# Loading and transposing the first four row tiles in halves of the contraction, under a new plan

## Chip, cores, metric

One core of one Trainium2 chip. The time is device microseconds (us) of one execution; lower is better. The kernel before takes 316.13 us (median of 4 runs, 315.47 to 316.74).

## The reference

```python
# x: 16 x 512 x 1024, w1 and w2: 1024 x 768, all float32
def reference(x, w1, w2):
    y1 = np.matmul(x, w1)
    y2 = np.matmul(x, w2)
    return (np.tanh(y1) * y2).astype(np.float32)
```

## The kernel before

The 64 row tiles (128 rows each) are worked in two ways. The first six, the *head*, are multiplied directly while the weights still arrive. The other 58 go in 29 pairs (numbered 0 to 28) through a scheme with seven block products in place of eight; that is the *steady part*, which begins at about 44 us. Its x tiles are loaded, cast and transposed by the DMA (a *transposing transfer*). A plan in the kernel fixes the order of the work on each engine and in the DMA queue that SyncE issues ("dma"). In the plan `Lx0` loads row tile 0, `La0` a row block of w1, `T00` and `T01` transpose the two halves of tile 0 on TensorE, `m00F3` is a head product, `st0` stores a head tile, `Lp70`, `Tx70` load and transpose the first tile of pair 7, `store0.5` stores a steady result, `p1.0` and so on are steady products.

```python
    WARM = 21                     # filler matmuls while the first loads run
    LOADS = ("x0 a0 x1 a1 x2 a2 x3 a3 a4 a5 a6 a7 b0 b1 b2 b3 b4 b5 b6 b7").split()
    EARLY = ("La0", "La1", "La2", "La3")      # issued by ACT, the rest by SyncE
    FILL = {"m00F0": 3, "m00F1": 6}           # fillers on ones, ahead of these
    ORDER = {
        "pe": """
            T00 T01 m00F0 m00G0 T10 T11 m00F1 m00G1 m10F0 T20 m10G0 m10G1 m10F1 T21 ...
        """,
        # ... "act", "dve" ...
        "dma": """
            Lx0 La0 Lx1 La1 Lx2 La2 Lx3 La3 La4 La5 La6 La7 Lb0 Lb1 Lb2 Lb3 Lb4 Lx4 Lb5 Lb6 Lx5 Lb7 Lp00 Lp01
            Lp10 Lp11 Tx00 Lp20 Tx01 st3 Lp21 Tx10 Lp30 st4 Tx11 Lp31 st1 Tx20 Lp40 Lp41 Tx21 st2 Lp50 Tx30
            Lp51 Tx31 Lp60 st5 Tx40 Lp61 st0 Tx41 Lp70 store1.5 Tx50 store0.5 Lp71 Tx51 store0.1 store1.1 Tx60
            store0.7 store1.7 Tx61 store1.3 store0.3 store0.9 store1.9
        """,
    }
    # ...
    def load_head_x(mt, h=None):
        if mt not in hf:
            hf[mt] = xfpool.tile([P, K], f32, tag="xf", name="x_f")
        cols = slice(0, K) if h is None else slice(h * K // 2, (h + 1) * K // 2)
        pin(nc.sync.dma_start(hf[mt][:, cols], xf[mt][:, cols]))
    # ...
    # past the plan, by slots of 0.65 us (one product):
    for i in range(FIRST, PAIRS):
        z = 14 * i - 6
        # ...
        late = 1.1 * (i == FIRST + 1)
        for h in range(2):
            at(slot(z - 24 + (1 + h) * late + 4 * h), cast_x, i, h, "dve")
            at(slot(z - 24 + (1 + h) * late + 4 * h), transpose_x, i, h)
```

Of the kernel before, what the change touches and what calls it, by code (L numbers as in the profile page):

```python
# [13 lines left out]
def kernel(  # L14
# [739 lines left out]
```

## Time and profile before

| | before |
|---|---|
| span of the profiled run | 314.2 us |
| first transposition on TensorE | 6.21 us |
| first steady product | 43.94 us |
| TensorE lost between there and 46.63 (worked out in the prediction) | 0.75 us |
| idle TensorE from 46.63 to 310.5 | 0.03 us |

TensorE is the bound, so the table is read as a sum: when does the steady part begin, and what does TensorE wait for from there on? The lines are in the prediction below.

### The profile page before, as it was taken

The page shows a single profiled execution, that of the slowest core. Times are in us where ns is not written, and L with a number is a line of the kernel's source. Part 1 is how long each engine was busy: PE and PEld are TensorE (multiplying, and loading weights), DVE is VectorE, ACT ScalarE, POOL GpSimd, SP SyncE. Part 2 cuts the span into 40 slices and gives each one's busy share as a digit, 9 for nine tenths or more (in the row PEclk, how much of TensorE's full clock was granted, in tenths as well). Part 3 has the DMA queues.
Part 4 walks back from the last instruction along what each step waited for, and adds up shares of the span by engine and source line. Part 5 has one row for each costly group of instructions (what it writes and reads, how often), then busy time and mean ns, then how long its engine had stood idle before and what let it go on. Part 6 is the DMA issues. An engine that isn't in the chain of part 4 may idle for free.

```text
span 314.2 us, 5489 instructions
## 1 busy us (share of the span) xinstructions
PE 307.3 (98%) x1893; PEld 185.6 (59%) x1898; DVE 244.8 (78%) x571; ACT 230.5 (73%) x453; POOL 4.3 (1%) x10
## 2 busy tenths in 40 slices
PE   7999999999999999999999999999999999999995
PEld 5756656666656555555555556555555555555662
DVE  1688988888788778877777887777788777778653
ACT  3798879787888777778777777877777787776552
POOL 0000000000000000000000000000000000000004
PEclk9999999999999999999999999999999999999999
DMA  7999398999999999999999989999998989985322
GB/s 276 407 399 381 78 310 237 271 299 258 290 288 310 297 272 231 228 294 266 285 240 252 273 253 225 291 252 259 253 251 281 260 256 271 237 256 126 144 103 100
DMA packets 82300, 80.59 MB, mean 256 GB/s; under 512 B 63584, under 2 KB 64096, under 8 KB 82272
## 3 DMA queue, kind: packets, MB, share of 16 engines
q1 hardware_dynamic: 81552, 78.46, 88.0%
q10 hardware_dynamic: 720, 1.77, 1.4%
q8 instruction: 15, 0.25, 0.3%
q14 instruction: 13, 0.11, 0.1%
HBM read 39.85 MB, written 25.17 MB: 207 GB/s over the span
## 4 chain that ended last, share of the span: by engine, by line
PE 89%; DMA 8%; DVE 1%; issue 1%; ACT 0%; ACTq 0%; SPq 0%; DVEq 0%
PE bank L401 84%; DMA wf<-in_w_dram 8%; PE bank L267 3%; PE bank L270 2%; DVE t L318 1%; DVE s L382 1%; PE bank L238 0%; DVE o L437 0%; ACT o L283 0%; ACTq L250 0%; SPq L250 0%; ACT junk L260 0%; PE bank L300 0%; DVE o L287 0%; DVE out_r L390 0%
## 5 line engine op out<-in xcount | busy, mean ns | idle before, releaser
L401 PE MATMUL bank<-t,s 128*128 128x384 f16 x696 | 131.5, 326 | 0.4 <-DVE t L318 0.4
L401 PEld LDWEIGHTS <-s 128*128 128x128 f16 x928 | 90.7, 98 | 61.1 <-issue 0.8
L401 PEld LDWEIGHTS <-xT 128*128 128x128 f16 x696 | 68.0, 98 | 46.7 <-issue 0.9
L401 PE MATMUL bank<-b,xT 128*128 128x384 f16 x464 | 93.7, 326 | 0.0
L423 DVE TENSOR_TENSOR c<-bank,u 128x384 f32<-128x384 f32 x58 | 31.9, 553 | 41.1 <-PE bank L401 39.6
L340 ACT ACTIVATE junk<-x_f 128x1024 bf16<-128x1024 f32 x58 | 60.8, 1049 | 2.4 <-DMA x_f<-in_x_dram 2.4
L431 ACT ACTIVATE th<-c,out_r 128x384 f32<-128x384 f32 x58 | 35.3, 609 | 21.1 <-DVE c L423 21.1
L401 PE MATMUL bank<-b,s 128*128 128x384 f16 x232 | 47.0, 326 | 0.0
L401 PE MATMUL bank<-t,xT 128*128 128x384 f16 x232 | 46.9, 325 | 0.0
L418 ACT ACTIVATE u<-bank 128x384 f32<-128x384 f32 x58 | 28.2, 487 | 20.0 <-PE bank L401 19.7
L360 DVE TENSOR_SCALAR x_h<-x_f,pr 128x1024 f16<-128x1024 f32 x55 | 41.0, 746 | 0.2
L431 ACT ACTIVATE th<-bank,out_r 128x384 f32<-128x384 f32 x58 | 33.3, 574 | 6.1 <-PE bank L401 6.1
L414 ACT ACTIVATE bank<-bank 128x384 f32<-128x384 f32 x58 | 27.9, 481 | 12.6 <-DVE o L437 10.0
L437 DVE SCALAR_TENSOR_TENSOR o<-bank,out_r,th 128x384 f32<-128x384 f32 x58 | 35.4, 610 | 2.0 <-PE bank L401 2.0
L423 DVE TENSOR_TENSOR c<-bank,s 128x384 f32<-128x384 f32 x58 | 32.1, 554 | 6.1 <-PE bank L401 5.0
L437 DVE SCALAR_TENSOR_TENSOR o<-c,out_r,th 128x384 f32<-128x384 f32 (+1 forms) x57 | 34.3, 606 | 0.4 <-ACT th L431 0.2
L418 ACT ACTIVATE s<-bank 128x384 f32<-128x384 f32 x58 | 27.9, 482 | 7.3 <-PE bank L401 5.1
L382 DVE TENSOR_TENSOR s<-xT 128x512 f16<-128x512 f16 x58 | 24.0, 416 | 0.2
L267 PE MATMUL bank<-wb,xTb 128*128 128x512 bf16 x91 | 23.6, 379 | 0.1
L270 PE MATMUL bank<-wb,xTb 128*128 128x256 bf16 x96 | 14.6, 273 | 0.1
L260 ACT ACTIVATE junk<-wf 128x768 bf16<-128x768 f32 (+1 forms) x13 | 12.8, 988 | 1.4 <-DMA wf<-in_w_dram 1.2
L267 PEld LDWEIGHTS <-xTb 128*128 128x128 bf16 x96 | 9.3, 99 | 7.5 <-DVE xTb L231 0.3
(49 smaller groups left out, 143.4 us busy)
## 6 DMA issues: line engine op xcount, KB each, us to landing
x_f<-in_x_dram SPq DMA_DIRECT2D x64, 512.0 KB, 5.8
out_dram<-o SPq DMA_DIRECT2D x62, 384.0 KB, 3.6
wf<-in_w_dram SPq DMA_DIRECT2D x12, 384.0 KB, 7.7
wf<-in_w_dram ACTq DMA_DIRECT2D x4, 384.0 KB, 8.5
xT<-x_h SPq DMA_TRANSPOSE x58, 3.7
out_dram<-o SPq DMA_DIRECT2D x3, 192.0 KB, 1.9
out_dram<-o ACTq DMA_DIRECT2D x1, 192.0 KB, 1.9
```

The costliest lines, as they stand in the source:

```text
L260: pin(nc.scalar.activation(junk[:, :n * N].rearrange("p (k n) -> p k n", n=N), w_f[t][:, k:k + n, :], ACT.Abs, accum_out=asum_w[t][:, j:j ...
L267: pin(nc.tensor.matmul(bank, hx[mt][:, k, :], w_b[t][k][:, :F], start=k == 0, stop=k == KO - 1))
L270: pin(nc.tensor.matmul(bank[:, at_:at_ + G], hx[mt][:, k, :], w_b[t][k][:, F:], start=k == 0 and mt % 2 == 0, stop=k == KO - 1, skip_group ...
L340: pin(nc.scalar.activation(junk[:, :K], xs[HEAD + 2 * i + h], ACT.Abs, scale=2.0 ** -12, accum_out=pair_sum[i][:, h:h + 1]))
L360: pin(nc.vector.tensor_scalar(xh, xs.pop(mt), pair_r[i][:, h:h + 1], None, ALU.mult))
L382: pin((nc.vector if eng == "dve" else nc.gpsimd).tensor_tensor(s, st[i, a], st[i, b], op))
L401: pin(nc.tensor.matmul(bank[:, cols], st[i, a][:, k, :], wt[t][b][:, k, cols], start=start and k == 0, stop=stop and k == KH - 1, skip_gro ...
L414: pin(nc.scalar.activation(ub[u]["b"][:, :Q], ub[u]["a"][:, :Q], ACT.Copy))
L418: pin(nc.scalar.activation(c, ub[u][bank][:, :Q], ACT.Copy))
L423: pin(nc.vector.tensor_tensor(c, ub[u][bank][:, :Q], ub[u][other], ALU.add))
L431: pin(nc.scalar.activation(th, v, ACT.Tanh, scale=rs[i][:, 0, h:h + 1]))
L437: pin(nc.vector.scalar_tensor_tensor(o[:, h, q * Q + cols.start:q * Q + cols.stop], v, rs[i][:, 1, h:h + 1], tanhs[i, h, q][:, cols], ALU. ...
```

## The change

The intent: a row tile's load of 512 KB becomes two of 256 KB, one for each half of the contraction, and the four first halves are loaded ahead of the four second ones. TensorE can then transpose and multiply first halves with the first weight blocks about 0.7 us earlier. A new plan for all engines and for the DMA queue comes with it. The diff, cut to its core:

```diff
-    WARM = 21
+    WARM = 15
-    LOADS = ("x0 a0 x1 a1 x2 a2 x3 a3 a4 a5 a6 a7 b0 b1 b2 b3 b4 b5 b6 b7").split()
+    LOADS = ("x00 a0 x10 a1 x20 a2 x30 a3 x01 a4 x11 a5 x21 a6 x31 a7 b0 b1 b2 b3 b4 b5 b6 b7").split()
-    FILL = {"m00F0": 3, "m00F1": 6}
+    FILL = {"T10": 5, "T20": 3}
     "pe":
-            T00 T01 m00F0 m00G0 T10 T11 m00F1 m00G1 m10F0 T20 m10G0 m10G1 m10F1 T21 ...
+            T00 T10 m00F0 m00G0 T20 m10F0 m10F1 m10G0 m10G1 T30 m00G1 m00F1 T01 m00F2 m10G2 m00G2 m10F2 m20F0
+            T11 m20F1 m20G0 m20F2 m20G1 m20G2 m20G3 m20F3 T21 ...
     "act", around the start of the steady part:
-            ... tanh4G ax20 cx11 b11b b22b seed.0 seed.1 s5.0 u2.0 ax21 ...
+            ... tanh4G b22b b11b cx11 seed.0 ax21 s5.0 seed.1 u2.0 ax20 ...
     "dma":
-            ... Tx00 Lp20 Tx01 st3 Lp21 Tx10 Lp30 st4 Tx11 Lp31 st1 Tx20 Lp40 Lp41 Tx21 st2 Lp50 Tx30 ...
+            ... Tx00 Lp20 Tx01 Lp21 st0 Tx10 st4 Lp30 Tx11 Lp31 Tx20 Lp40 Lp41 Tx21 Lp50 st1 Tx30 ...
     # (other lines of the plan, the dependencies of the halves: cut)
-            pin(nc.tensor.transpose(banks[6 + h][:, k * P:(k + 1) * P],
+            pin(nc.tensor.transpose(banks[6 + mt % 2][:, k * P:(k + 1) * P],
-            op(f"L{what}", "dma", STEP[what], n - 200, [], load_head_x, i)
+            op(f"L{what}", "dma", STEP.get(what, 0.72), n - 200, [], load_head_x, i, int(what[2]))
```

More of the change, by code (lines that the diff above doesn't have):

```diff
@@ L58 @@
     ELSEWHERE = {
-        "e01": "dve", "e11": "dve", "e20": "act", "e21": "dve", "e31": "dve", "ca0": "act", "ca1": "act",
-        "cb4": "act", "b22a": "dve", "cx11": "act", "cx31": "act", "cx61": "act"
+        "e10": "act", "e21": "dve", "e31": "dve", "cb4": "act", "b22a": "dve", "cx11": "act", "cx31":
+        "act", "cx41": "act", "cx61": "act"
     }
-    FILL = {"m00F0": 3, "m00F1": 6}
+    FILL = {"T10": 5, "T20": 3}
     ORDER = {
         "pe": """
-            T00 T01 m00F0 m00G0 T10 T11 m00F1 m00G1 m10F0 T20 m10G0 m10G1 m10F1 T21 m20G0 m20F0 m20F1 m20G1
-            m10G2 m20G2 m00F2 m00G2 m20F2 m10F2 T30 T31 m10G3 m00G3 m20F3 m10F3 m20G3 m00F3 m10F4 m10G4 m20F4
-            m20G4 m00G4 m00F4 m30G0 m30G1 m30G2 m30G3 m20G5 m10G5 m10F5 m20F5 m20G6 m10G6 m10F6 m30G4 m30G5
-            m30G6 m20G7 m10G7 m30G7 m10F7 m00F5 m00F6 m00F7 suma m11F0 m20F6 m20F7 m01F0 m00G5 m00G6 m00G7
-            m11F1 m01F1 m30F0 m30F1 m30F2 m30F3 m30F4 m30F5 m30F6 m30F7 m21F0 m21F1 m11F2 m21F2 m01F2 m11F3
-            m21F3 m01F3 m31F0 m31F1 m31F2 m31F3 m21G0 m21G1 m21G2 m21G3 m31G0 m31G1 m31G2 m31G3 m01F4 m31G4
-            m21G4 m11F4 m01G0 m01G1 m11G0 m11G1 m01G2 m01G3 m01G4 m31F4 T4 m11F5 m11F6 m01F5 m31F5 m01G5 m01G6
-            m31F6 m01F6 m31G5 m31G6 m01F7 m31F7 m11F7 m31G7 T5 m40F0 m40F1 m40F2 m40F3 m40F4 m40F5 m40F6 m01G7
-            m40F7 m21G5 m21G6 m50F0 m50F1 m50F2 m50F3 m50F4 m50F5 m50F6 m50F7 m21F4 m21F5 m21G7 m21F6 m21F7
-            m11G2 m11G3 m11G4 m11G5 m11G6 m11G7 m40G0 m50G0 m50G1 m50G2 m50G3 m50G4 m50G5 m50G6 m50G7 m40G1
-            m40G2 m40G3 m40G4 m40G5 m40G6 m40G7 sumb m41F0 m41F1 m41F2 m41F3 m41F4 m41F5 m41F6 m41F7 m41G0
-            m41G1 m41G2 m41G3 m41G4 m41G5 m41G6 m51G0 m51G1 m51G2 m51G3 m51G4 m51G5 m51G6 m51G7 m41G7 m51F0
-            m51F1 m51F2 m51F3 m51F4 m51F5 m51F6 m51F7 p1.0 p1.1 p5.0 p6.0 p2.0 p3.0 p7.0 p5.1 p6.1 p4.0 p2.1
-            p7.1 p1.2 p3.1 p4.1 p1.3 p6.2 p2.2 p5.2 p6.3 p2.3 p5.3 p7.2 p7.3 p3.2 p4.2 p3.3 p4.3 p1.4 p1.5
-            p5.4 p5.5 p2.4 p6.4 p6.5 p2.5 p7.4 p7.5 p3.4 p3.5 p4.4 p4.5 p1.6 p1.7 p5.6 p6.6 p2.6 p6.7 p2.7
-            p7.6 p3.6 p5.7 p7.7 p4.6 p3.7 p1.8 p4.7 p1.9 p2.8 p6.8 p5.8 p5.9 p7.8 p1.10 p3.8 p4.8 p3.9 p6.9
@@ new lines @@
+            T00 T10 m00F0 m00G0 T20 m10F0 m10F1 m10G0 m10G1 T30 m00G1 m00F1 T01 m00F2 m10G2 m00G2 m10F2 m20F0
+            T11 m20F1 m20G0 m20F2 m20G1 m20G2 m20G3 m20F3 T21 m00G3 m00F3 m10F3 m10F4 m00F4 m20G4 m00G4 m20F4
+            T31 m30G0 m30G1 m30G2 m30G3 m00G5 m00F5 m20G5 m30G4 m30G5 m00F6 m20G6 m00G6 m30G6 m30G7 m20G7
+            m00G7 m10G3 m10G4 m10F5 m10F6 m10F7 m10G5 suma m20F5 m10G6 m10G7 m30F0 m20F6 m20F7 m11F0 m11F1
+            m11F2 m01F0 m01F1 m01F2 m31F0 m31F1 m31F2 m00F7 m30F1 m30F2 m30F3 m30F4 m30F5 m30F6 m30F7 m11F3
@@ new lines @@
+            m11F4 m01F3 m01F4 m31F3 m21G0 m31G0 m21G1 m21G2 m21G3 m21G4 m01G0 m01G1 m01G2 m01G3 m01G4 m11G0
+            m11G1 m21F0 m21F1 m21F2 m21F3 T4 m21F4 m21G5 m01G5 m01G6 m01F5 m11F5 m01F6 m01F7 m21G6 m21G7 m11G2
+            m11G3 m11G4 m11G5 m11G6 m31G1 m31G2 m31G3 m40F0 m40F1 m21F5 m21F6 m21F7 m11F6 m11F7 T5 m31F4 m31F5
+            m31F6 m31F7 m40F2 m40F3 m40F4 m40F5 m40F6 m40F7 m50F0 m50F1 m50F2 m50F3 m50F4 m50F5 m40G0 m40G1
+            m40G2 m50G0 m11G7 m01G7 m50F6 m50F7 m40G3 m40G4 m40G5 m40G6 m40G7 m31G4 m31G5 m50G1 m50G2 m50G3
@@ new lines @@
+            m50G4 m50G5 m50G6 m50G7 sumb m41F0 m41F1 m41F2 m41F3 m41F4 m41F5 m41F6 m41F7 m31G6 m31G7 m41G0
+            m41G1 m51G0 m41G2 m41G3 m41G4 m41G5 m41G6 m41G7 m51G1 m51G2 m51G3 m51G4 m51G5 m51G6 m51G7 m51F0
+            m51F1 m51F2 m51F3 m51F4 p1.0 p1.1 p5.0 p2.0 p6.0 p5.1 m51F5 m51F6 p6.1 p7.0 p3.0 p7.1 p4.0 m51F7
+            p3.1 p2.1 p4.1 p1.2 p1.3 p5.2 p5.3 p6.2 p2.2 p6.3 p2.3 p7.2 p7.3 p3.2 p4.2 p3.3 p4.3 p1.4 p1.5
+            p5.4 p6.4 p2.4 p2.5 p6.5 p5.5 p7.4 p7.5 p3.4 p4.4 p3.5 p4.5 p1.6 p1.7 p5.6 p5.7 p6.6 p2.6 p6.7
@@ L81 @@
+            p2.7 p7.6 p7.7 p3.6 p4.6 p3.7 p4.7 p1.8 p1.9 p5.8 p6.8 p2.8 p5.9 p7.8 p1.10 p3.8 p4.8 p3.9 p6.9
             p2.9 p2.10 p7.9 p5.10 p4.9
@@ L83 @@
         "act": """
-            ca0 absa0 ca1 absa1 e20 absa2 absa3 absa4 absa5 absa6 absa7 tanh2G absb0 tanh1F tanh0G tanh2F cb4
-            tanh0F absb2 absb6 tanh3F absb4 ax00 absb7 ax01 b21a tanh4F tanh5F ax10 ax11 tanh4G ax20 cx11 b11b
-            b22b seed.0 seed.1 s5.0 u2.0 ax21 b21b u2.1 f00.0 s5.1 f10.0 ax31 seed.2 ax30 seed.3 f11.0 u2.2
-            u2.3 s5.2 s5.3 f00.2 f01.0 ax40 cx31 f10.2 seed.4 ax41 seed.5 s5.4 s5.5 u2.4 u2.5 f11.2 f00.4 ax51
-            f01.2 ax50 f10.4 seed.6 f11.4 seed.7 f01.4 u2.6 s5.6 ax61 u2.7 s5.7 f00.6 f11.6 f10.6 seed.8 ax60
@@ L89 @@
-            f00.8 u2.8 f01.6 s5.8 cx61 s5.9 seed.9 f10.8 seed.10 u2.9 f01.8 f11.8 f00.10 s5.10
+            absa0 e10 absa1 absa2 e01 absa3 e11 absa4 absa5 absa6 absa7 tanh2G absb0 tanh0G b21a cb4 tanh2F
+            tanh0F tanh1F absb2 absb4 absb7 tanh3F ax00 ax01 absb6 tanh4F ax10 tanh5F ax11 tanh4G b22b b11b
+            cx11 seed.0 ax21 s5.0 seed.1 u2.0 ax20 u2.1 s5.1 b21b f00.0 f10.0 ax31 f11.0 f01.0 seed.2 seed.3
+            ax30 u2.2 u2.3 s5.2 s5.3 f00.2 ax41 f10.2 ax40 seed.4 cx31 seed.5 u2.4 f01.2 f11.2 u2.5 s5.4 s5.5
@@ L90 @@
+            f00.4 ax51 cx41 f10.4 seed.6 f01.4 ax50 seed.7 f11.4 u2.6 u2.7 s5.6 s5.7 f00.6 ax61 f11.6 f10.6
+            seed.8 ax60 f01.6 u2.8 f00.8 s5.8 s5.9 cx61 seed.9 f10.8 seed.10 u2.9 f01.8 f11.8 f00.10 s5.10
         """,
         "dve": """
-            e00 e01 e10 e11 ca2 e21 ca3 ca4 e30 ca5 ca6 e31 ca7 parta cb0 cb1 scalea b11a cb2 cb3 t1a b22a hx4
-            cb6 cb5 t2a e41 cb7 hx5 mul0F mul3F mul1F e51 t3a rx0 cx00 cx01 mul2G mul2F mul0G partb t4a rx1
-            cx10 scaleb mul4F sx0 mul4G s1.0 s2.0 s4.0 s3.0 sx1 t1b t2b t3b c22.0 rx2 sx2 cx20 t4b s1.1 c22.1
@@ L95 @@
-            f00.1 s2.1 c12.0 f10.1 s3.1 cx21 c12.1 s4.1 f11.1 rx3 cx30 c22.2 c22.3 s3.2 s1.2 f00.3 f01.1 c12.2
-            c12.3 s2.2 f10.3 mul5F rx4 cx40 s4.2 cx41 s3.3 c22.4 f11.3 c22.5 f00.5 s1.3 c12.4 f01.3 s2.3 f10.5
-            rx5 f11.5 s4.3 cx50 c12.5 f01.5 c22.6 sx3 cx51 c22.7 f00.7 s1.4 s2.4 sx4 s3.4 c12.6 c12.7 rx6 cx60
-            s4.4 sx5 f01.7 c22.8 f10.7 f11.7 s1.5 s2.5 c12.8 s3.5 c12.9 f00.9 c22.9 s4.5 f11.9 f01.9 f10.9
+            e00 ca0 ca1 e20 ca2 e30 ca3 ca4 ca5 e21 ca6 e31 ca7 cb0 parta cb1 scalea cb2 b22a cb3 b11a t1a t2a
@@ new lines @@
+            hx4 cb5 cb6 cb7 e41 mul0F hx5 t3a t4a mul1F e51 rx0 cx00 mul3F partb mul2F mul0G cx01 scaleb sx0
+            rx1 cx10 mul4F mul2G mul4G s1.0 s3.0 s2.0 t1b t2b s4.0 t3b rx2 c22.0 cx20 c22.1 t4b s1.1 f00.1
+            c12.0 c12.1 f10.1 s2.1 cx21 sx1 s3.1 s4.1 rx3 cx30 f11.1 c22.2 c22.3 s1.2 mul5F f00.3 c12.2 s2.2
+            s4.2 f10.3 rx4 f01.1 c12.3 s3.2 sx2 cx40 f11.3 c22.4 c22.5 s1.3 f00.5 c12.4 f01.3 c12.5 s2.3 s4.3
+            f10.5 s3.3 f01.5 rx5 cx50 s3.4 f11.5 sx3 c22.6 c22.7 cx51 f00.7 sx4 s1.4 c12.6 s2.4 s4.4 c12.7
@@ L99 @@
+            f11.7 rx6 cx60 f01.7 c22.8 f10.7 c12.8 s1.5 s2.5 s4.5 s3.5 sx5 f00.9 c12.9 c22.9 f01.9 f10.9 f11.9
         """,
         "dma": """
-            Lx0 La0 Lx1 La1 Lx2 La2 Lx3 La3 La4 La5 La6 La7 Lb0 Lb1 Lb2 Lb3 Lb4 Lx4 Lb5 Lb6 Lx5 Lb7 Lp00 Lp01
-            Lp10 Lp11 Tx00 Lp20 Tx01 st3 Lp21 Tx10 Lp30 st4 Tx11 Lp31 st1 Tx20 Lp40 Lp41 Tx21 st2 Lp50 Tx30
-            Lp51 Tx31 Lp60 st5 Tx40 Lp61 st0 Tx41 Lp70 store1.5 Tx50 store0.5 Lp71 Tx51 store0.1 store1.1 Tx60
-            store0.7 store1.7 Tx61 store1.3 store0.3 store0.9 store1.9
+            Lx00 La0 Lx10 La1 Lx20 La2 Lx30 La3 Lx01 La4 Lx11 La5 Lx21 La6 Lx31 La7 Lb0 Lb1 Lb2 Lb3 Lb4 Lx4
@@ L105 @@
+            Lb5 Lx5 Lb6 Lb7 Lp00 Lp01 Lp10 Lp11 Tx00 Lp20 Tx01 Lp21 st0 Tx10 st4 Lp30 Tx11 Lp31 Tx20 Lp40 Lp41
+            Tx21 Lp50 st1 Tx30 st5 Lp51 Tx31 store0.1 st3 Tx40 Lp60 st2 Tx41 Lp61 store0.5 Tx50 Lp70 store1.5
+            Tx51 store1.1 Lp71 Tx60 store0.7 store1.7 Tx61 store1.3 store0.3 store0.9 store1.9
         """,
@@ L230, in evacuate_f @@
         if eng == "dve":
-            pin(nc.vector.tensor_copy(dst, banks[6 + h]))
+            pin(nc.vector.tensor_copy(dst, banks[6 + mt % 2]))
         else:
-            pin(nc.scalar.copy(dst, banks[6 + h]))
+            pin(nc.scalar.copy(dst, banks[6 + mt % 2]))
     def pe_transpose_b(mt, bank):
@@ L526, in op2 @@
         op(name, engine, COST[kind, engine], due, needs, fn, *args, engine)
-    STEP = {"x0": 2.2, "a0": 0.3, "x1": 1.75, "a1": 0.8, "x2": 1.4, "a2": 0.8, "x3": 1.6, "a3": 0.2}
+    STEP = {"x00": 1.35, "a0": 0.1, "x10": 1.5, "a1": 0.1, "x20": 1.5, "a2": 0.1, "x30": 1.5, "a3": 0.1}
     for n, what in enumerate(LOADS):
@@ L537 @@
         for h in range(2):
-            op(f"T{mt}{h}", "pe", 0.45, 4.5 + 2.3 * mt + 0.1 * h, [f"Lx{mt}", f"e{mt - 1}{h}" if mt else ""], pe_transpose_f, mt, h)
-            op2("e", f"e{mt}{h}", ("dve", "act")[h], 4.6 + 2.3 * mt + 0.1 * h, [f"T{mt}{h}", f"e{mt}0" if h else "", f"e{mt - 1}0" if mt and not h else ""],
+            op(f"T{mt}{h}", "pe", 0.45, 4 + 1.6 * mt + 5 * h, [f"Lx{mt}{h}", f"e{mt - 2}{h}" if mt > 1 else f"e{mt + 2}0" if h else ""],
+               pe_transpose_f, mt, h)
+            op2("e", f"e{mt}{h}", ("dve", "act")[h], 4.1 + 1.6 * mt + 5 * h, [f"T{mt}{h}", f"e{mt}0" if h else "", f"e{mt - 1}0" if mt and not h else ""],
                 evacuate_f, mt, h)
@@ L547 @@
                 op(f"abs{a}{k}", "act", 0.23 + 0.82 * n, 8 + 1.3 * k + 17 * t, [f"L{a}{k + n - 1}"], abs_w, t, k, n)
-    held = {6: "e30", 7: "e31"}
+    held = {6: "e21", 7: "e31"}
     def accumulate(m, t, which, bank, due):
@@ L598 @@
             scales(1, 5, 36)
+    if HEAD == 4:
+        scales(1, 5, 36)
     for m in (0, 2):
@@ L627 @@
             r = HEAD + n - 6
-            x_free = f"e{r}1" if r < 4 else f"hx{r}" if r < HEAD else f"cx{(r - HEAD) // 2}{r % 2}"
+            x_free = "" if r < 0 else f"e{r}1" if r < 4 else f"hx{r}" if r < HEAD else f"cx{(r - HEAD) // 2}{r % 2}"
             h_free = f"Tx{(n - 4) // 2}{n % 2}" if n >= 4 else f"T{HEAD - 4 + n}" if HEAD - 4 + n >= 4 else ""
```

## The prediction

> **What bounds the kernel now.** I read the page first: its busy shares, then its slices.
>
> ```profile
> span 314.2 us, 5489 instructions
> PE 307.3 (98%) x1893; PEld 185.6 (59%) x1898; DVE 244.8 (78%) x571; ACT 230.5 (73%) x453; POOL 4.3 (1%) x10
> ...
> PE   7999999999999999999999999999999999999995
> ```
>
> TensorE is busy in every slice but the first and the last. The change touches only the start, so the question is where the start ends and what TensorE loses in it. I took the busy time of PE in six stretches whose borders come from the timeline: first transposition (6.21), third row tile's transposition (10.52), first steady product (43.94), end of the last wait (46.63), last product (310.5). Columns: stretch, length, PE busy (instructions), granted clock, DMA share, GB/s.
>
> ```profile
> 0.00:6.21 6.21, 3.99 (x22) 1.00 0.71 239
> 6.21:10.52 4.31, 3.96 (x29) 1.00 1.03 418
> 10.52:43.94 33.42, 33.21 (x220) 1.00 0.88 308
> 43.94:46.63 2.69, 2.27 (x14) 1.00 0.96 277
> 46.63:310.50 263.87, 263.84 (x1612) 1.00 0.91 249
> 310.50:314.20 3.70, 0.00 (x0) 1.00 0.43 159
> ```
>
> From 46.63 on there is no gap: 263.9 us of products that the change leaves alone, and 3.7 us of output. So the span moves only by what moves the border at 46.63. Between 10.52 and 43.94 only 0.2 us is idle, although the head's loads run to about 30 us. What can be won lies before 10.52 and between 43.94 and 46.63. Busy is not useful there, as the timeline of PE shows (start, length, what, idle before it):
>
> ```profile
> 6.21 1.06 PE L223 MATMUL bank<-ident,x_f 128*128 128x128 f32 x8 [1.18 <-DMA x_f<-in_x_dram]
> 7.11 0.49 PE L153 MATMUL bank<-ones 128*128 128x256 bf16 x3
> ...
> 8.27 1.09 PE L223 MATMUL bank<-ident,x_f 128*128 128x128 f32 x8 [0.15 <-DMA x_f<-in_x_dram]
> 9.20 0.82 PE L153 MATMUL bank<-ones 128*128 128x256 bf16 x6
> ...
> 10.52 0.66 PE L223 MATMUL bank<-ident,x_f 128*128 128x128 f32 x4 [0.18 <-DMA x_f<-in_x_dram]
> ```
>
> Each row tile is waited for, and L153 is filler on ones that keeps the array busy: 9 x 0.108 = 1.0 us of no use. At the other border I read ACT beside PE:
>
> ```profile
> 41.08 1.06 ACT L340 ACTIVATE junk<-x_f 128x1024 bf16<-128x1024 f32 x1 [1.68 <-DMA x_f<-in_x_dram]
> ...
> 42.14 1.13 ACT L362 ACTIVATE x_h<-x_f,pr 128x1024 f16<-128x1024 f32 x1
> 43.18 3.03 ACT L313 ACTIVATE b<-wf,wp1r 128x1536 f16<-128x1536 f32 x2
> ...
> 46.11 0.84 ACT L414 ACTIVATE bank<-bank 128x384 f32<-128x384 f32 x2
> 46.63 0.81 PE L401 MATMUL bank<-t,s 128*128 128x384 f16 x4 [0.38 <-DVE t L318]
> ```
>
> The profile names DVE's t (it ended at 46.59), but this product reads the first weight set's t2, made long before, and adds to the bank that ACT's seed (L414, 46.11 to about 46.5) writes; the built program has it wait for ACT. So ACT is the cause: 1.68 us idle for a late x tile, a cast, then two weight blocks before the seed. PE loses some 0.2 us (products that need the first of those blocks) and 0.54 us (45.44 + 4 x 0.1625 = 46.09 to 46.63): about 0.75 us.
>
> **What the Trainium skill says.** "DMA: Bandwidth & Descriptors", section Specifications: a ceiling of 435 GB/s, full rate from 512 B up. The trace agrees on the first, 393 to 446 GB/s in half-microsecond slices from 4 us on; halved rows are 2 KB, above the second, and no run here shows it yet. Same page, section "Anatomy of one DMA": a fixed cost of about 2 us, most of it after the last byte. The trace: the first x tile and weight row block (917 KB) were moved by 4.8 us (mean 191 GB/s from 0), and their first users ran at 6.21 and 6.28, 1.4 us later. Same page, "Queues, rings and completion order": each DMA engine takes turns between the queues. The trace agrees: x (one queue) and weights (the other) come in pairs, 6.21/6.28, 8.27/8.81, 10.52/11.07. "TensorE: Matmul & The Clock Gate", section "What's actually happening": an idle array runs at half clock until some 3.4 us of activity. The trace agrees: the first fillers take 393 to 422 ns, the last six (from 4.2 us) 272 or 273, after 3.2 us of filling.
>
> **The change, part by part.**
>
> *Loads.* The pair is 256 + 384 KB instead of 512 + 384, so 655 KB instead of 917. From the cumulative bytes of the trace (160 GB/s to 4.2 us is 672 KB; 226 to 5.8 is 1.31 MB; 268 to 7.37 is 1.97 MB; then about 0.41 MB per us) plus the lag seen for x (1.41, 1.22, 1.27 us), the first halves land at 5.5, 7.05, 8.6 and 10.2 us. The second halves, each behind one more weight block: 10.8, 12.4, 14.0, 15.7. The last block of the first weights lands at 17.1, as before (the bytes are the same). One oddity in the built order: eight DMA semaphores are shared, SP now issues five x halves ahead, so ACT's fourth weight load waits for the first to land, and the 1.28 us table load stands behind it: ACT is free at 5.5 + 0.45 + 1.28 = 7.2 instead of 4.0. After one abs (0.84 + 0.19) it makes the second tile's copy (0.59), ready at 8.9. PE uses it only behind the third transposition, at about 9.0. No cost.
>
> *TensorE's early order.* Four transpositions are 0.43 us, a 512-column product 0.216, a 256-column one 0.108 (spacings in the trace). T00 5.5 to 5.9; T10 7.05 to 7.5; one block's products 0.33, to 7.8; T20 8.6 to 9.0; four products 0.65, to 9.7; T30 10.2 to 10.65; two products, to 11.0; T01 to 11.4; five products 0.87, to 12.3; T11 12.4 to 12.9; seven products 1.08, to 14.0; T21 to 14.4; eight products 1.40, to 15.8; T31 to 16.3. Useful work by then: 8 x 0.43 + 15 x 0.216 + 13 x 0.108 = 8.1 us. So it is as if PE had worked without a gap from 16.3 - 8.1 = 8.2. The kernel before, by the same count: total useful work from the first transposition to 43.94 is 96 x 0.216 + 96 x 0.108 + 32 x 0.107 + 16 x 0.056 + 0.3 for the sums = 35.8 us, and 43.94 - 35.8 = 8.1. The 0.7 us that the first half gains by coming earlier is spent waiting for the next halves, because the new order does little with the products that already could run between them. Front: -0.3 to +0.5, say +0.1 us.
>
> *16 to 43 us.* The same products in another order. DVE makes five head copies instead of seven and eight weight casts instead of six: near balance. Banks 4, 0 and 2 come free after tanh instructions that ACT reaches some us before PE needs them. I allow +0.1 us for gaps that I do not see.
>
> *The border to the steady part.* ACT now makes the two weight blocks right after the last head tanh, ahead of the cast and of the abs that waited 1.68 us; three 512-column head products (0.65 us) are kept back and put between the first steady products. The seed then waits only for its own product. Of the 0.75 us lost I expect 0.5 to be saved, since DVE's first s blocks move behind two more head multiplications (0.69 us each).
>
> *Filler.* 15 + 8 instead of 21 + 9, all in time in which PE would wait. Worth nothing by itself.
>
> Sum: +0.1 + 0.1 - 0.5 = -0.3 us.
>
> **The rivals.**
> 1. *The early half pays in full:* the first transposition comes 0.7 us earlier, all of it reaches the end, and the border saves 0.75: -1.5 us, 314.7. For it: first halves offer more work per byte (four tiles against four blocks after 2.6 MB, 16 products of each width; before, 2.75 MB gave 9). Against it: the order puts only three products of each width ahead of the fourth tile's transposition, and PE is full after 10.5 in either kernel.
> 2. *A cold array:* 15 fillers end just at 4.2, where the clock was seen to switch, and are followed by 1.3 us of waiting and then thin work. If the array stays at half clock into the dense part, each 3.4 us there costs 1.7: +1 to +2 us, 317.5. Against it: before, 1.2 us of waiting and 0.8 us of filler per 2 us kept it warm.
> 3. *ACT or DVE becomes the bound at the border:* the second tile's fp16 cast of the first pair now stands behind three more DVE instructions, its transfer-transposition lands 3.7 us after issue, and the s blocks wait for it: +0.5 us instead of -0.5, 316.7. For it: DVE was 4.9 of 5 us busy from 35 to 40.
>
> **Range and chances.** Before was 316.16 (315.47 to 316.74 in three runs), so half a microsecond is noise. Less 0.3 gives 315.8. Rival 1 sets the lower end with the noise, 314.6; rivals 2 and 3, damped by their odds, the upper end, 317.2. Two per cent is 6.3 us. All that PE loses before 46.63 is 1.9 + 0.75 us and the start at 6.21, so a gain of 6.3 us is out of reach; a loss of that size needs several stalls of a kind that I do not see. Faster 0.01, same 0.975, slower 0.015.
>
> **What would show it right or wrong.** Right: first transposition at 5.3 to 5.7; T30 at about 10.2 with waits for x before it; T31 ending near 16.3; no idle of note from there to the first steady product at about 43.3 to 43.6; no wait of more than 0.2 us among the first steady products; steady stretch again 263.9 us. Front wrong: x halves landing 0.5 us off my times, or DVE's copies, not DMA, being what the transpositions wait for. Rival 2: transpositions spaced 0.21 us instead of 0.107 after 6 us. Rival 3: PE waiting for ACT or DVE between 42 and 48 us. Steady part wrong: products of more than 0.1625 us, which nothing in the change should cause.

## The result, and the profile after

The changed kernel takes 317.58 us (median of 4 runs, 317.24 to 317.84). The ratio to the kernel before is 1.0046, with a 95% interval of 1.0023 to 1.0068: slower by 0.5%, "same" by a limit of 2%, but 1.8 us above the predicted value and above the top of the range, 317.2. Ratios here are the mean time of one kernel's fast runs over that of the other's in the same rounds, so not quite the ratio of the medians quoted.

The page of the kernel after, its span, busy time and slices of TensorE:

```profile
span 315.6 us, 5482 instructions
...
PE 308.7 (98%) x1891; PEld 185.6 (59%) x1891; DVE 244.2 (77%) x570; ACT 231.3 (73%) x454; POOL 4.3 (1%) x10
...
PE   7999999999999899999999999999999999999995
```

The busy share is the same 98%. One digit is new: the 8 in the 14th slice (102.6 to 110.5 us), far from anything that the diff speaks of. The windows of PE after follow; their borders are the starts of T00 and T30, the end of T31, the first steady product, a point 34 products later, and the last product. Columns as in the prediction: stretch, length, PE busy (instructions), clock, DMA share, GB/s.

```profile
0.00:5.11 5.11, 3.39 (x16) 1.00 0.58 166
5.11:10.03 4.92, 4.92 (x27) 1.00 1.02 391
10.03:17.14 7.11, 6.44 (x45) 1.00 1.04 397
17.14:44.37 27.23, 27.23 (x184) 1.00 0.86 263
44.37:50.11 5.74, 5.74 (x36) 1.00 1.09 334
50.11:312.00 261.89, 260.86 (x1594) 1.00 0.92 249
312.00:315.60 3.60, 0.16 (x1) 1.00 0.44 164
```

Three readings. The wait at the start of the steady part is gone (5.74 of 5.74 busy). The first steady product comes at 44.37, and as the new plan keeps three head products of 0.217 us back for later, that is worth 45.02 against 43.94 before: 1.08 us later for equal work. And the steady part now has a hole of 1.03 us. The timeline of the transpositions after (start, length, what, idle before it):

```profile
5.11 1.09 PE L223 MATMUL bank<-ident,x_f 128*128 128x128 f32 x4 [0.69 <-DMA x_f<-in_x_dram]
7.05 1.10 PE L223 MATMUL bank<-ident,x_f 128*128 128x128 f32 x4
8.94 0.60 PE L223 MATMUL bank<-ident,x_f 128*128 128x128 f32 x4
10.03 0.60 PE L223 MATMUL bank<-ident,x_f 128*128 128x128 f32 x4
11.54 0.63 PE L223 MATMUL bank<-ident,x_f 128*128 128x128 f32 x4 [0.59 <-DVE xTb L231]
13.12 0.63 PE L223 MATMUL bank<-ident,x_f 128*128 128x128 f32 x4
14.78 0.63 PE L223 MATMUL bank<-ident,x_f 128*128 128x128 f32 x4
16.70 0.60 PE L223 MATMUL bank<-ident,x_f 128*128 128x128 f32 x4
```

First halves come at 5.11, 7.05, 8.94, 10.03, the second ones at 11.54, 13.12, 14.78, 16.70; the prediction had 5.5, 7.05, 8.6, 10.2 and 11.0, 12.4, 14.0, 15.8. The first two take 1.09 us for what takes 0.60 later: the array was still on half clock (the clock column reads 1.00 there all the same, so it does not show this). DVE is named ahead of the fifth one (T01), because a copy of DVE ended at 11.43; but a DMA issue in SyncE's queue that waits on the load of x01 is released at 11.43 too. It was the load: in after_warm21 the record names it (0.41 us before 11.47), and in after_again T01 starts at 11.42 while the same copy of DVE runs from 11.37 to 12.06.

The hole is in the chain of waits after (start, length, what), and in the timelines of PE and DVE at the same place:

```profile
98.18 7.13 DMA xT<-x_h
...
105.33 0.04 DVE s L382
...
107.07 2.94 PE bank L401 x17
```

```profile
107.07 0.81 PE L401 MATMUL bank<-t,xT 128*128 128x384 f16 x4 [1.03 <-DVE c L423]
```

```profile
105.33 0.42 DVE L382 TENSOR_TENSOR s<-xT 128x512 f16<-128x512 f16 x1 [1.17 <-DMA xT<-x_h]
```

DVE waits for a transposing transfer, the second of pair 7 (Tx71; the expectations below call that pair the seventh or, counting from one, the eighth), issued at 98.18 and landed 7.13 us later; DVE's sum is late, and with it what PE needs. SyncE's issue queue around it, before and then after:

```profile
93.15 1.44 SPq L368 DMA_TRANSPOSE xT<-x_h  x1
94.69 1.05 SPq L452 DMA_DIRECT2D out_dram<-o  x2
95.80 0.53 SPq L334 DMA_DIRECT2D x_f<-in_x_dram  x1
96.92 1.60 SPq L368 DMA_TRANSPOSE xT<-x_h  x1
```

```profile
93.90 1.23 SPq L368 DMA_TRANSPOSE xT<-x_h  x1
95.19 1.64 SPq L452 DMA_DIRECT2D out_dram<-o  x3
96.87 1.20 SPq L334 DMA_DIRECT2D x_f<-in_x_dram  x1
98.18 1.87 SPq L368 DMA_TRANSPOSE xT<-x_h  x1
```

Tx71's data are cast by DVE at 96.10 to 96.85 before and 96.49 to 97.24 after. Before, the transfer is issued 0.07 us after its cast; after, it stands 0.94 us behind three stores instead of two and a load that takes 1.20 us to issue instead of 0.53. It also takes longer from issue to landing, 7.13 us instead of 6.8. The two differences, 0.87 and 0.33 us, add up to about the 1.17 us that DVE waits. Before, there was no slack either: Tx71 landed at 103.7 (96.92 + 6.8), and DVE took it at 103.72.

So the profile's account of the 1.4 us (315.6 - 314.2) is: +1.08 to the first steady product, some -0.7 at the border (before, 0.75 lost; after, 0.1 at most), +1.03 at 106 us. Together +1.4. This is one look at each kernel. Two other profiles have the first loads and the head of the kernel before unchanged, and their first steady products come at 43.67 (before_dma) and 43.02 us (before_act); the seven with the changed head lie at 44.25 to 44.56. So the front costs 1.1 us in this pair, and up to 2 us against the other looks.

### The profile page after: what moved, and what is told of

It is laid out like the page before. It is cut to its first block, busy times and chain, and to the rows that moved or that the text cites. A ratio compares the mean times of both kernels' runs of the same rounds, so it can differ in the third digit from the quotient of the medians.

```text
span 315.6 us, 5482 instructions
## 1 busy us (share of the span) xinstructions
PE 308.7 (98%) x1891; PEld 185.6 (59%) x1891; DVE 244.2 (77%) x570; ACT 231.3 (73%) x454; POOL 4.3 (1%) x10
## 4 chain that ended last, share of the span: by engine, by line
PE 94%; DMA 4%; DVE 1%; issue 0%; DVEq 0%
PE bank L401 82%; PE bank L267 6%; PE bank L270 3%; DMA xT<-x_h 2%; PE bank L223 1%; DMA x_f<-in_x_dram 1%; DVE xTb L231 0%; PE bank L153 0%; PE bank L238 0%; DVE c L423 0%; DVE o L437 0%; DVE s L382 0%; DVE wb L254 0%; PE bank L300 0%; DVEq L437 0%
## 5 line engine op out<-in xcount | busy, mean ns | idle before, releaser
L360 DVE TENSOR_SCALAR x_h<-x_f,pr 128x1024 f16<-128x1024 f32 x54 | 40.3, 746 | 0.5 <-DVE pr L350 0.3
L267 PE MATMUL bank<-wb,xTb 128*128 128x512 bf16 x96 | 25.0, 382 | 0.0
L270 PE MATMUL bank<-wb,xTb 128*128 128x256 bf16 x96 | 13.9, 274 | 0.0
```

Of the source, the lines that this page charges most:

```text
L267: pin(nc.tensor.matmul(bank, hx[mt][:, k, :], w_b[t][k][:, :F], start=k == 0, stop=k == KO - 1))
L270: pin(nc.tensor.matmul(bank[:, at_:at_ + G], hx[mt][:, k, :], w_b[t][k][:, F:], start=k == 0 and mt % 2 == 0, stop=k == KO - 1, skip_group ...
L360: pin(nc.vector.tensor_scalar(xh, xs.pop(mt), pair_r[i][:, h:h + 1], None, ALU.mult))
```

## The experiments

Two theories to begin with. *Front:* loads slowed by the halves or an array gone cold made the first steady product late. *Steady:* the order of the queue made Tx71 late, and it costs its full length. The rivals are named with each run. One identity helps to read them. For every kernel with the changed plan, span less first steady product less the wait at 106 us (or just after) is a constant:

| kernel | first steady product | wait | span | rest |
|---|---|---|---|---|
| after | 44.37 | 1.03 | 315.6 | 270.20 |
| after_again | 44.25 | 0.57 | 314.9 | 270.08 |
| after_warm21 | 44.37 | 0 | 314.6 | 270.23 |
| after_store | 44.51 | 1.08 | 315.8 | 270.21 |
| after_nostore | 44.40 | 1.55 | 316.2 | 270.25 |
| after_pe | 43.81 | 1.19 | 315.1 | 270.10 |
| after_dma | 44.35 | 0.84 | 315.6 | 270.41 |
| after_t71 | 44.56 | 1.14 | 315.9 | 270.20 |
| after_pe_t71 | 43.85 | 0 | 314.1 | 270.25 |
| after_best | 43.79 | 0 | 314.0 | 270.21 |

The rest is the same to 0.17 us but for one run. So these two numbers are the whole difference among these kernels, and the wait costs what it is long. It also differs from one execution to the next (the same kernel: 1.03 and 0.57). One profile therefore does not show what an edit did to it: by the same sum, with the first steady product held fixed, the six spans of after_warm21 (314.6 to 315.9) leave 0 to 1.3 us for it, an estimate.

### after_again: the changed kernel once more

> The changed kernel itself, so that its parts can be compared on the same chip. If the loss is systematic: 1.4 us over the kernel before (ratio about 1.0045), and in the profile again a wait of about 1 us of TensorE near 106 us (for the seventh pair's second transposed tile, which took 7.1 us from issue to landing), a half-speed array until about 8.6 us, and loads at about 305 GB/s between 4.5 and 6 us against 400 before. If the wait near 106 us was an accident of one profiled execution, it is missing here and the ratio stays.

317.42 us, ratio 1.005 (1.0034 to 1.0066), profiled wait 0.57 us. The slowdown is real and repeats.

### after_warm21: is it the cold array?

```diff
-    WARM = 15
+    WARM = 21
```

> The changed kernel with 21 warm-up matmuls again instead of 15. Cold-array theory: the array was at half speed from 5.1 to 8.6 us[...]; with 21 it is at full speed from the first transposition on, and if that cost what it looks like (0.43 us for each of two transpositions, 0.5 for the five fillers, 0.3 for two products) the end comes about 1 us earlier: ratio to before about 1.001. Load theory: TensorE has to wait for the fifth half tile at about 11.4 us anyway, so all that a fast array gains before is lost in that wait: within 0.2 us of the changed kernel, ratio about 1.0045, though the first transpositions take 0.43 us.

317.07 us, ratio 1.0038 (1.0022 to 1.0054). The array is warm from the second transposition on:

```profile
5.49 0.78 PE L223 MATMUL bank<-ident,x_f 128*128 128x128 f32 x4
7.08 0.66 PE L223 MATMUL bank<-ident,x_f 128*128 128x128 f32 x4 [0.27 <-DMA x_f<-in_x_dram]
```

Still the first steady product comes at 44.37, exactly as in the changed kernel. What the cold array lost had been hidden in the wait for x01. The profiles taken for other purposes say the same: of eight with 15 fillers, four have a first transposition of 1.09 us and four of 0.63, and within the same matmul order the first steady product is not earlier where the array was warm (44.35 to 44.56 us against 44.25 to 44.40). Rival 2 of the prediction is out. The wait at 106 us was near zero in this profiled run, the fastest of six, with no cause in the edit: Tx71 was issued at 98.31, later than in the changed kernel, but landed after 5.90 us instead of 7.13.

### before_cols, before_rows, before_half_order, before_half_alt: what slows the first loads

From 4 to 6.5 us the changed kernel's loads run slower than those of before. Four versions of the kernel *before*, with its plan, change only how x0 to x3 are loaded (the last two also put these loads at the head of the plan):

```diff
 # in load_head_x, for mt < 4
+  before_cols:        two column halves of a tile, one right after the other
+  before_rows:        two halves of 64 partitions, whole 4 KB rows
+  before_half_order:  x00 x10 x20 x30 x01 x11 x21 x31   (all first halves ahead)
+  before_half_alt:    x00 x11 x20 x31 x01 x10 x21 x30   (jumping between tiles too, halves alternating)
```

> The kernel before with each of the first four x tiles loaded in two halves of its columns (2 KB rows) one right after the other; plan and order unchanged. Short-row theory: the DMA engines move 2 KB rows more slowly while the first loads run, so the rate between 4 and 6.5 us falls from about 400 to about 310 GB/s, by 6.5 us about 1.35 MB are moved instead of 1.6 to 1.75, and the head ends some 0.5 us later (ratio about 1.002, less what the earlier first transposition gives). If the new order of the loads or the changed plan is to blame, the rate stays near 400.

> The kernel before with each of the first four x tiles loaded in two halves of its partitions (64 rows of 4 KB each): as many loads as in the run with halves of columns, but long rows. Short-row theory: the rate between 4 and 6.5 us stays near 400 GB/s, 1.6 to 1.75 MB by 6.5 us. Load-count theory (issue time and the eight shared semaphores hold the queue back): the rate falls to about 310 as in the changed kernel.

> The kernel before with its own plan, but x00 to x3 loaded as column halves with all four first halves ahead of the four second ones, as in the changed kernel. The loads of the first 6.5 us ran at some 240 GB/s in the kernel before and with adjacent halves, at 200 to 208 in every kernel with the changed plan. If the order of the halves alone slows them: from 4 to 6.5 us some 310 GB/s instead of 390 to 420, and 1.3 MB by 6.5 us instead of 1.6. If what slows them is something else in the changed plan (queue shares with the weights, semaphores): some 400 GB/s. Time by itself says little here, since the first tile is complete only with its second half: 317 to 319 us.

> As before_half_order, but the eight halves alternate between first and second columns while they still jump from tile to tile. If it is the same columns of every row (only every second 2 KB piece of the memory) that slow the loads: some 400 GB/s from 4 to 6.5 us. If it is the jump from tile to tile: some 310, as with all first halves ahead. If neither order slows anything: 400 in both.

The windows of 4.00 to 6.50 us, last column GB/s: before, before_cols, before_half_alt, before_half_order, after.

```profile
4.00:6.50 2.50, 1.32 (x11) 1.00 1.01 407
```

```profile
4.00:6.50 2.50, 2.10 (x13) 1.00 1.05 409
```

```profile
4.00:6.50 2.50, 2.50 (x12) 1.00 1.04 404
```

```profile
4.00:6.50 2.50, 1.81 (x12) 1.00 0.91 291
```

```profile
4.00:6.50 2.50, 1.81 (x9) 1.00 0.91 322
```

Halved rows of 2 KB alone cost nothing (409), nor does jumping between tiles (404). The loads are slow where several first halves follow each other (291, 322; 306 in after_again). So it is the order of the halves, not their size. Why it is slower is not shown; each order had one profiled look or two. All ten profiles with the changed plan lie at 199 to 208 GB/s from 0 to 6.5 us, the three with whole tiles at 247 to 266. By 6.5 us the changed kernel has moved 1.33 MB against 1.61 MB (6.5 us by the windows' 204 and 247 GB/s), which is 0.7 us at some 405 GB/s; after that the rates are alike (394 to 402 GB/s in both from 11.5 to 17.2 us), so the lag stays. No run gave the changed kernel another order of its loads, so that its front recovers with one is not shown. The time of before_cols was 316.76 us, ratio 1.0017 (0.998 to 1.0055).

before_rows took 322.27 us (ratio 1.0181) and the two others 321.5 and 322.0 in one look each, all with the clock taken back to half for some microseconds between 8 and 17 us (a mean granted clock of 0.51 to 0.64 from 8 to 15 us), during or after a wait of TensorE of 3.8 to 5.6 us for complete tiles. Their times say nothing about the loads, and before_rows is confounded altogether: 64-partition loads ran at 217 to 350 GB/s themselves.

### after_pe: the order of the early matmuls

```diff
-  ... T30 m00G1 m00F1 T01 m00F2 m10G2 m00G2 m10F2 m20F0 T11 m20F1 ...
+  ... T30 m00G1 m00F1 m20G0 m20F0 m20F1 m20G1 T01 m00F2 m10G2 m00G2 m10F2 m20F2 m20G2
+      T11 m30F0 m30G0 m30F1 m30G1 m30F2 m30G2 ...
```

> The changed kernel with TensorE's order alone changed between 10.5 and 20 us: ten products of the third and fourth tile that could already run are put ahead of the transpositions of the second halves, where TensorE waits for x (0.64 + 0.25 + 0.11 us in the profile). Order theory (loads are late, and the plan leaves ready products idle): the steady part starts about 0.9 us earlier, ratio about 1.002. If the front is bound by the weight blocks that land until 17.3 us, the gain is lost again before 20 us and the ratio stays at 1.0045.

317.28 us, ratio 1.0027 (1.0002 to 1.0052). Four products that were ready fill the wait ahead of T01 and six the one ahead of T21, and the first steady product comes at 43.81, some 0.5 us earlier. The wait at 106 us was 1.19 us: Tx71 landed 0.5 us earlier than in the changed kernel (104.79), but DVE came to it 0.7 us earlier (103.48). The prediction's remark that the new order does little with ready products holds, and is worth 0.5 us at the border.

### after_store and after_nostore: one store less ahead of it, less traffic

```diff
 after_store:   the transposing transfer of pair 7, first tile, 0.3 slots later, so that one store goes ahead of it
-            at(slot(z - 24 + (1 + h) * late + 4 * h), transpose_x, i, h)
+            at(slot(z - 24 + (1 + h) * late + 4 * h + 0.3 * (i == FIRST + 1 and h == 0)), transpose_x, i, h)
 after_nostore: two head stores dropped (a wrong result, on purpose)
-        pin(nc.sync.dma_start(of[mt], ho[mt // 2][:, mt % 2, :]))
+        if mt not in (0, 4):
+            pin(nc.sync.dma_start(of[mt], ho[mt // 2][:, mt % 2, :]))
```

> The changed kernel with one output store put back where the kernel before has it: two stores instead of three stand between the seventh pair's two transfer-transpositions. If the third store is what makes the second transposition land late (at 105.3 us), the wait of 1.03 us near 106 us goes away and the end comes 1.0 us earlier: ratio to before about 1.001. If the transposition is late because the whole load and store sequence is late, or the wait only moves to the next store, the gain is under 0.3 us.

> The changed kernel without the stores of head rows 0 and 4 (two of the first stores, 768 KB; a wrong result on purpose, those rows are not written). Backlog theory: the DMA queue is full from 40 to 105 us and never makes up what it lost earlier (about 0.36 MB less than before was moved by 90 us), so the seventh pair's transposed tile lands late; without 0.79 MB of stores it lands 1 to 2 us earlier, the wait of 0 to 1.1 us near 106 us is gone in every profile, and the end comes about 0.6 us earlier than the changed kernel (ratio about 1.003). If the wait comes from when the transposition is issued (its cast, its buffers) and not from the queue, it stays.

317.46 us and 318.0 us, ratios 1.005 and 1.0049; the waits were 1.08 and 1.55 us. Neither two stores between the transfers in place of three nor 768 KB less to move in the head removed it. Neither theory's forecast came true. A backlog of bytes from the head is out. The one store is not settled: in after_store Tx71 was still issued at 98.01 us, 0.74 after its cast, so the edit hardly moved it.

### after_dma and before_dma: the old queue order in the new kernel, and the reverse

```diff
 after_dma: from Tx00 on, the order of before
-  Tx00 Lp20 Tx01 Lp21 st0 Tx10 st4 Lp30 Tx11 Lp31 Tx20 Lp40 Lp41 Tx21 Lp50 st1 Tx30 ...
+  Tx00 Lp20 Tx01 st0 Lp21 Tx10 Lp30 st4 Tx11 Lp31 st1 Tx20 Lp40 Lp41 Tx21 st5 Lp50 Tx30 ...
 before_dma: the mirror image
```

> The changed kernel with the kernel before's order of the loads, stores and transposing transfers from the first transposing transfer on. If the order in that queue makes the wait at 106 us (theory): the wait for the second transposed tile of the seventh pair is under 0.2 us and the time 0.5 to 1 us shorter than the changed kernel's 317.4, so 316.4 to 316.9, ratio to before 1.0015 to 1.0035. Rival (the lateness of the front and of what frees the buffers makes it, not the order): the wait stays at 0.6 to 1.1 us, ratio 1.005.

> The mirror: the kernel before with the changed kernel's order of loads, stores and transposing transfers in the same stretch. If the order makes the wait: a wait of 0.5 to 1 us near 105 us and a time of 316.4 to 316.9, ratio 1.0015 to 1.0035. Rival: no wait there, ratio 0.999 to 1.001.

after_dma: 318.04 us, ratio 1.0063 (1.0032 to 1.0094), wait 0.84 us: no help. But the edit did not restore the place of Tx71, which lies past the plan: three stores and a load still stand between the two transfers of pair 7 (95.64 to 98.43 us). The first of them now landed late as well (DVE waited 1.57 us for it until 97.64), so the cast of Tx71 ended at 98.73 and its issue came at 98.79. This run is thus no test of the order there. before_dma: 316.73 us, ratio 1.0009 (0.9982 to 1.0035), with three stores in that place (94.38 us) instead of two, and the wait appears in a kernel that shows none in the profiles of before, before_act and before_cols, all with two:

```profile
105.99 0.81 PE L400 MATMUL bank<-t,xT 128*128 128x384 f16 x4 [0.57 <-DVE c L422]
```

So the new order came with a wait without the new front, in one profile. The time of before_dma is not separated from before.

### after_t71, after_pe_t71, after_best: Tx71 put first

```diff
 # when the planned events are sorted, between the two transposing transfers of pair 7:
+        later = [e for e in queue[a:b] if e[2] in (store, load_x)]
+        queue = queue[:a] + [e for e in queue[a:b] if e not in later] + queue[b:b + 1] + later + queue[b + 1:]
 after_pe_t71: after_pe with this;  after_best: the same with WARM = 21
```

> The changed kernel, with the second transposing transfer of the eighth pair put directly behind the first one in the queue, ahead of the three stores and the load that stand between them. In the changed kernel it was issued at 98.18 us, although its data were cast at 97.24: the queue was busy with those four. If its place in the queue makes the wait (theory): issued by 97.3, landed by 104.4 instead of 105.31, the wait at 106 us falls from 0.6 to 1.1 us to under 0.2, and the time from 317.4 to 316.6 to 316.9 (ratio 1.002 to 1.003). Rival (the transfers as a whole are behind, and a place in the queue is worth nothing): it lands at 105 again and the wait stays, ratio 1.005.

> The same on the version whose matmul order closes the first gap (first product of the steady part 0.5 us earlier, a gain that the wait at 106 us took back). Theory: the wait falls from 1.2 us to 0.3 to 0.6, as the landing comes 0.9 us earlier, and the time from 317.3 to 316.4 to 316.7 (ratio 1.0015 to 1.003). Rival: wait of 1.2 us as before, ratio 1.003 or more.

> The same with 21 instead of 15 filling matmuls at the start as well. Alone they moved nothing before the border to the steady part. Theory: as the run before within 0.3 us, ratio 1.001 to 1.003. If it beat the kernel before (ratio under 1), something in the reading of the front is wrong.

after_t71 took 317.31 us, ratio 1.0029 (1.0014 to 1.0044). The wait at 106 us is gone: DVE's sum starts at 104.16 without idle time ahead of it. But another has come 3 us later. SyncE's queue, DVE, ACT and PE of after_t71:

```profile
93.99 4.63 SPq L372 DMA_TRANSPOSE xT<-x_h  x2
98.67 2.51 SPq L456 DMA_DIRECT2D out_dram<-o  x3
101.22 1.92 SPq L338 DMA_DIRECT2D x_f<-in_x_dram  x2
```

```profile
104.16 0.42 DVE L386 TENSOR_TENSOR s<-xT 128x512 f16<-128x512 f16 x1
```

```profile
107.82 1.06 ACT L344 ACTIVATE junk<-x_f 128x1024 bf16<-128x1024 f32 x1 [1.24 <-DMA x_f<-in_x_dram]
```

```profile
109.87 1.46 PE L405 MATMUL bank<-t,s 128*128 128x384 f16 x8 [1.14 <-ACT u L422]
```

The 4.63 us are not the work of issuing: each transfer takes 1.25 us, and between them SyncE waits 2.1 us for DVE's cast of Tx71, with the stores and the load behind it. So the load goes out at 101.22 instead of 96.87, ACT idles 1.24 us for it, and PE 1.14 us for ACT. What the place in the queue did to Tx71 is plain in these times (us; "needed" is when DVE had nothing else left to do):

| kernel | cast ends | issued | issue to landing | needed | wait of PE near 106 |
|---|---|---|---|---|---|
| before | 96.85 | 96.92 | 6.8 | 103.60 | 0 |
| after | 97.24 | 98.18 | 7.13 | 104.16 | 1.03 |
| after_again | 97.02 | 98.11 | 6.52 | 103.95 | 0.57 |
| after_warm21 | 97.13 | 98.31 | 5.90 | 104.06 | 0 |
| after_t71 | 97.32 | 97.38 | 4.1 | 104.16 | 0 |
| after_pe_t71 | 96.61 | 96.67 | 4.5 | 103.45 | 0 |

Put first, Tx71 is issued with its cast and lands in 4.1 to 4.5 us instead of 5.9 to 7.13 (7.74 in after_nostore), over two microseconds before it is needed. Where the stores and the load go ahead of it, it lands 0.1 us after it is needed or later; and in the three profiles with the new plan and that order, issued within 0.2 us of each other, the time to landing decides between 0 and 1.03 us of waiting. The theory was right about what made the wait and wrong about the gain: here what one transfer gains another loses. The profiled execution of after_t71 was the slowest of six; two others, with spans of 314.6 and 314.7, leave no room for either wait by the sum above, so the new wait is not there every time.

after_pe_t71 took 316.68 us (ratio 1.0022, 1.0009 to 1.0035) and has no wait of PE in its steady part; ACT waits only 0.24 us for the same load. Its first steady product:

```profile
43.85 1.46 PE L405 MATMUL bank<-b,xT 128*128 128x384 f16 x8
```

after_best took 316.12 us, ratio 1.0002 (0.9988 to 1.0016). The changed kernel with another matmul order, Tx71 put first and 21 fillers is level with the kernel before, not faster. Between after_pe and after_pe_t71 the profiled spans differ by 1.0 us, the ratios by less than their intervals.

### before_act: the border alone

```diff
-  ... tanh4G ax20 cx11 b11b b22b seed.0 seed.1 s5.0 u2.0 ax21 b21b ...
+  ... tanh4G b11b b22b cx11 seed.0 seed.1 s5.0 u2.0 ax20 ax21 b21b ...
```

> The kernel before with one thing of the new plan alone: at the border to the steady part ScalarE makes the two second-set weight blocks ahead of the abs that waits for a late x tile. Prediction's step: TensorE's lost 0.75 us there becomes under 0.2, the end 0.5 to 0.7 us earlier, ratio 0.998. Rival: the first steady products then wait for VectorE's blocks (s, t of the second set) or for the second pair's later cast, and the gain is under 0.2 us.

This does one part of the change, ACT's order at the border, in the kernel before. 315.2 us (314.91 to 316.59), ratio 0.999 (0.9971 to 1.001). The profiled span is 313.1 us; PE's only wait in the steady part is this one of 0.36 us, for ACT's third weight block, which now stands behind the two moved tiles:

```profile
50.05 0.81 PE L401 MATMUL bank<-b,xT 128*128 128x384 f16 x4 [0.36 <-ACT b L313]
```

It is the fastest version of all by median and by profile, but its interval holds 1, so that it beats the kernel before is not shown (in the same rounds the kernel before had spans from 313.0 to 314.4). The edit did not save what the prediction gives this step, either. The 0.75 us at the border are gone (36 of these products from 43.02 to 48.87, 0.1625 us each), but 0.53 us are lost right behind them (48.87 + 4 x 0.1625 = 49.52, and the next starts at 50.05), so it nets 0.2 us. Most of the shorter span comes from a first steady product at 43.02 instead of 43.94, and there from loads that were faster before anything that was edited (266 against 247 GB/s to 6.5 us, first transposition at 5.49 instead of 6.21).

## Why the prediction was wrong

- *TensorE bounds, and only the start and waits count:* right. The identity above shows it: among these kernels nothing but the first steady product and one wait moved the span.
- *Loads and front, "+0.1 us":* mis-sized; this is the first failed step. The prediction took the bytes of the new loads at the rates of the kernel before. The first halves did come early (5.11 to 10.03), but with their order the loads ran at 322 instead of 407 GB/s from 4 to 6.5 us, and x01 landed about 0.6 us later than predicted. T31 ended at 17.14 instead of 16.3. By the prediction's own count (8.1 us of useful work by then) the front is worth a start without gaps at 9.0 instead of 8.2; before it was 8.1. The term is +0.9, not +0.1, for this pair of profiles. That the new order does little with ready products was right: after_pe won 0.5 us of it back.
- *16 to 43 us, "+0.1":* 45.02 - 9.04 - 35.8 = +0.2. Right. (The prediction's 35.8 adds up to 35.7 as written, which moves 0.1 us between these two terms; and one of its half-microsecond slices, 446 GB/s, lies above the 435 that it finds confirmed, so such slices hold to some 3%.)
- *The border, "-0.5":* right in kind, a little more in size: 0.1 of the 0.75 us is left at most, so about -0.7. ACT's order alone does not do it: in before_act 0.53 us of the loss came back a few products later. Which other part of the new plan kept it away in the changed kernel was not tested. Rival 3 did not happen.
- *"From 46.63 on there is no gap: 263.9 us of products that the change leaves alone":* the second failed step, and the term that was left out. The change also reorders the DMA queue, and in the steady part one transposing transfer landed late enough to stop PE for 0 to 1.5 us (1.03 in the profiled run). after_t71 shows that its place in the queue makes the wait: put first, it lands in 4.1 us instead of 7.13. The prediction looked at what the products read, not at how close the transfers that feed them were to being late: in the kernel before, Tx71 landed just as DVE came to it.
- *Rival 2, a cold array, 317.5:* nearly the right time by the wrong cause. The array was cold for the first two transpositions, but after_warm21 moved the first steady product by nothing.
- *Rival 1:* it did not happen; the second halves decided, as the prediction's text had it.

With the measured terms the sum is +0.9 + 0.2 - 0.7 + 1.0 = +1.4 us, as the spans have it (315.6 - 314.2). What stays open: why this order of halves is served more slowly; whether the later front adds to the lateness of Tx71 (before_dma had a wait without it; after_dma did not restore the order at that place); and why the same transfer takes 5.90 us in one execution and 7.13 in another, which is what makes the wait vary.

## What to carry to other kernels

A load rate belongs to an order of transfers: measure it for the new order before turning bytes into landing times. Where one in-order queue carries loads, stores and transposing transfers and the slack in it is below a microsecond, as here, a reordering at the start can show as a wait 60 us after it, so check the slack of each transfer (issue after its data are ready, landing before its reader) and not only whether PE waits now. Moving a transfer forward has a price in such a queue: until its data are ready, all that stands behind it waits too (2.1 us in after_t71). And a gain at one place is real only if the next late thing is later than the gain: after_pe's 0.5 us stood against a wait of 1.19 us, and only the profile with Tx71 moved too (after_pe_t71, span 314.1) shows it whole.

## What the Trainium skill lacked or had wrong

- "DMA: Bandwidth & Descriptors", Specifications, gives full rate from 512 B rows up. Rows of 2 KB agree when a tile's two halves are adjacent or alternate (409 and 404 GB/s), not when all first halves are loaded first (291 and 322). The same page's section "Latency and other measured facts" names slow row pitches, but from 512 KiB up; here the pitch is 4 KB, and no page has this case.
- The same page has no duration from issue to landing for a transposing transfer behind other traffic; here the same transfer took 7.13 us (98.18 to 105.31) behind three stores and a load, and 4.1 us ahead of them.
- "TensorE: Matmul & The Clock Gate", Part 4: PE-mode transpose, has some 275 ns for a 128 x 128 bf16 transposition in a kernel. The records here agree, in float32: the median of one is 273 ns. What the page lacks is how they follow each other: on a warm array four take 0.60 us and eight 1.04 us, so 0.11 us for each further one.
- The same page, section "What's actually happening", says that the time of the switch to full clock varies from run to run. The traces agree: with the same 15 fillers the first four transpositions took 1.09 us in four profiles and 0.63 in four others. No page says that this costs nothing where a later load is waited for anyway, as here.
